# The mixers' weight splits: ACT's negative and an adding DMA in place of a subtraction on DVE and GpSimd

## The chip, the cores and the metric

The kernel runs on one core of a Trainium2 chip. The metric is the device time of one execution in microseconds. One core has TensorE (PE, matrix multiplication; its weight loads are shown as PEld), VectorE (DVE), ScalarE (ACT), GpSimd (POOL) and SyncE (SP), each with its own instruction queue that is worked off in order. SP and POOL also issue DMA transfers, which sixteen DMA engines carry out.

## The reference, cut to what matters

The program is the trunk of a small decoder with 512 tokens of width 1024 and two layers. Each layer is: half a SwiGLU feed-forward block, a token mixer, half a SwiGLU block, all with RMSNorm before and after.

```
h = h + 0.5 * post(SwiGLU_a(pre(h)))
h = h + post(Mixer(pre(h)))
h = h + 0.5 * post(SwiGLU_b(pre(h)))
even layer: proj = u @ w_in  ->  dilated attention heads | gated DeltaNet heads  ->  @ w_out
odd  layer: proj = u @ w_in  ->  conv, SiLU, Mamba-2 chunked scan, gate, norm    ->  @ w_out
```

All data are float32. The change touches only how the weights of the two input projections `u @ w_in` are prepared.

## The kernel before, in words

**Products in split form.** TensorE multiplies in float32r, which keeps fewer bits than float32. So every operand is held as two parts, `hi` (the value rounded to float32r) and `lo` (the rest, value minus `hi`), and each product is three matmuls: hi·hi, hi·lo and lo·hi. One unit of weights is a tile of 128 partitions by 1024 numbers, 512 KB. `weights` (L88) takes such a unit through these steps: SP loads it from HBM into a tile `wraw` (`load`, L83; three buffers); ACT casts it into `whi` (L80); DVE subtracts, `wlo = wraw - whi` (L81). `whi` and `wlo` come from the pool `wsplit` with four buffers each. `product` (L159) then issues 24 matmuls for the unit, three for each of the eight blocks of rows (L167, L168, L169); the third of the first three, L169, is the first that needs `wlo`. A `wraw` buffer is free for the next load when the subtraction has read it; a `wsplit` buffer when the unit's last matmul is done.

**Sharing with GpSimd.** In the even mixer, from `self.share = True` (L899) to the end of the heads, every fifth subtraction goes to GpSimd instead of DVE.

**The even mixer** (L578 on) computes, between L899 and L929, the attention heads as a filler between the steps of the gated DeltaNet heads: 20 units of weights. Its longest serial piece is `invert32` (L693), 31 steps of a small multiplication and a reduction, both on DVE (L718, L719), by which a triangular matrix is inverted; meanwhile PE works at the attention (transposes L847 and L853, scores L831 and L832) and at further projections.

**The odd mixer** (L936 on) goes through four groups `g`. For each it projects B and C, then four blocks `i` of x, and then four gate blocks z: ten units, except that the first four units are made earlier, so 36 units in the loop. A projection ends in `conv_silu` (ACT L474, three DVE steps L476, ACT's tanh L478, DVE L479). For each block of x two decay tiles `M` (256 KB each) are read from a row in HBM by DMAs that **POOL** issues (L557), ACT works on them (L1062, L1065 four times, L1066), DVE multiplies (L1067), and PE takes them in L1072. There are four `M` buffers, so the loads for block `i+2` wait until PE is through with L1072 of block `i`. The transposes of a block of x into tokens are L1006.

**What sets the order.** The code is written stage by stage; a scheduler of the framework orders the instructions of each engine by priority and by its own estimate of when they can run, when the kernel is built. The order of each queue is then fixed.

Of the kernel before, what the change touches and what calls it, by code (L numbers as in the profile page):

```python
# [9 lines left out]
F32 = mybir.dt.float32  # L10
# [3 lines left out]
AF = mybir.ActivationFunctionType  # L14
OP = mybir.AluOpType
# [15 lines left out]
class Trunk:  # L31


    def __init__(self, ctx, tc, norm_w, tables, out):
        self.tc, self.nc, self.norm_w, self.tables, self.out = tc, tc.nc, norm_w, tables, out
        nc = self.nc
        pool = lambda name, **kw: ctx.enter_context(tc.tile_pool(name=name, **kw))
        self.consts = pool("consts", bufs=1)
        self.resid = pool("resid", bufs=1)
        self.wraw = pool("wraw", bufs=3)  # L40
        self.wsplit = pool("wsplit", bufs=4)
        self.scr = pool("scr", bufs=2)
        self.small = pool("small", bufs=4)
        self.dram = pool("dram", bufs=1, space=bass.MemoryType.DRAM)
        self.psum_mm = pool("psum_mm", bufs=2, space=bass.MemoryType.PSUM)
        self.psum_ctx = ctx.enter_context(ExitStack())
        self.banks({"acc": 4, "tr": 2})

        self.share, self.n_weights = False, 0
        self.ident = self.consts.tile([128, 128], F32, name="ident")  # L50
        make_identity(nc, self.ident)
        self.warm(24)
        self.h = self.resid.tile([128, TT, D], F32, name="h")
        self.uT = [self.resid.tile([128, TT, KD, 128], F32R, name=n) for n in ("uhi", "ulo")]
# [19 lines left out]
            return self.psum_mm.tile([128, 512], F32, name=tag)  # L74
        return self.psum.tile([128, 512], F32, name=tag, bufs=self.tags[tag])

    def split(self, src, hi, lo, on_pool=False):

        nc = self.nc
        nc.scalar.copy(hi, src)  # L80
        (nc.gpsimd if on_pool else nc.vector).tensor_tensor(lo, src, hi.bitcast(F32), op=OP.subtract)  # L81

    def load(self, src, shape):  # L83
        raw = self.wraw.tile([128] + shape, F32, name="wraw")
# [3 lines left out]
    def weights(self, src, shape, parts=None, raw=None):  # L88

        nc = self.nc  # L90
        raw = self.load(src, shape) if raw is None else raw
        hi, lo = parts or [self.wsplit.tile([128] + shape, F32R, name=x) for x in ("whi", "wlo")]
        self.n_weights += 1
        self.split(raw, hi, lo, self.share and self.n_weights % 5 == 0)
        return hi, lo

    def w_cols(self, w, c0, n=128, raw=None):
# [474 lines left out]
    def even_mixer(self, w_in, conv_w, a_log, dt_bias, head_norm_w, w_out, post_w, next_pre):  # L572
        nc, tc = self.nc, self.tc
# [7 lines left out]
        with ExitStack() as ctx:  # L581
# [314 lines left out]
                finish(*waiting)  # L896
                yield 1.5

            self.share = True  # L899
            fill = attention()  # L900
            for need in gated_delta():
                while need > 0:
# [23 lines left out]
                            nc.sync.dma_start(self.h[:, i, :], hd[i])  # L926
                    yield

            self.share = False  # L929
            parts.close()  # L930
            self.out_product(ctx, lambda t, k, half: [u[:, t, k, :] for u in self.uT], w_out, KD, 1.0, post_w, next_pre,
                             before=gates(pool("even_z", bufs=2)))
# [3 lines left out]
    def odd_mixer(self, w_in, conv_w, conv_b, dt_bias, a_log, d_skip, out_norm_w, w_out, post_w, next_pre):  # L936
        nc, tc = self.nc, self.tc
# [10 lines left out]
        with ExitStack() as ctx:  # L948
# [29 lines left out]
            with tc.tile_pool(name="odd_t", bufs=1, reuse_waits="tile") as tp:  # L978
                first = (DI // 128, DI // 128 + NG, 0, 1)
                ps, raw = self.first_products(w_in, [X0 + j * 128 for j in first], "acc",  # L980
                                              lambda: self.small_product(tp, w_in[:, DT0:DT0 + NH], NH, ("acc", "tr")))
# [11 lines left out]
            def project(j, tag="feat", bufs=2):  # L993
                p = first.get(j)
                if p is None:
                    p = self.ps("mm")
                    self.product(p, self.w_cols(w_in, X0 + j * 128))
                o = gp.tile([128, T], F32, name=tag, bufs=bufs)
                self.conv_silu(p, [cw[:, k * nconv + j:k * nconv + j + 1] for k in range(4)],
                               cw[:, 4 * nconv + j:4 * nconv + j + 1], o, gp)  # L1000
                return o
# [7 lines left out]
            def rstd_cols(g, sq):  # L1009

                p = self.ps("tr")[:, :TT]
                for t in range(TT):
                    nc.tensor.matmul(p[:, t:t + 1], sq[:, t * 128:(t + 1) * 128], self.ones[:, :1], start=True, stop=True)
                ss = self.small.tile([128, TT], F32, name="ssy")
                nc.vector.tensor_copy(ss, p)
                rms[g] = self.rstd(ss, 4 * GW, 0.5)
# [11 lines left out]
                    self.split(blocks(y[:, i, :]), *(o[:, :, g % 2 * NB + i, :] for o in (early if g < 2 else self.uT)))  # L1028

            ready, rms = {}, {}  # L1030
            for g in range(NG):
                Bf, Cf = project(DI // 128 + g), blocks(project(DI // 128 + NG + g, "Cf", 2))
                bt = gp.tile([128, TT, 128], F32, name="bt")
# [64 lines left out]
                for i in range(NB):  # L1098
# [7 lines left out]
                    if i:  # L1106
                        tt(sq, sq, th, op=OP.add)
                ready[g] = y
            rstd_cols(NG - 1, sq)

            for g in (NG - 2, NG - 1):
# [7 lines left out]
def kernel(  # L1119
# [29 lines left out]
    for layer in range(depth):  # L1149
        ffn = [(ffn_w_gate[layer, i], ffn_w_up[layer, i], ffn_w_down[layer, i]) for i in range(2)]  # L1150
        mixer, weights = (k.odd_mixer, odd) if layer % 2 else (k.even_mixer, even)
        k.ffn(*ffn[0], (layer, 1), (layer, 2), *(() if layer else (raws,)))
        mixer(*(w[layer // 2] for w in weights), (layer, 3), (layer, 4))
        k.ffn(*ffn[1], (layer, 5), (layer + 1, 0) if layer + 1 < depth else None)
# [47 lines left out]
```

## Time and profile before

| | |
|---|---|
| median of 3 runs | 2156.76 us (2154.38 to 2159.07) |
| the profiled execution | 2155.31 us, of which the span from the first to the last instruction 2153.5 us |
| PE busy | 2112.7 us (98%) |
| DVE busy | 1479.1 us (69%) |
| ACT busy | 1026.2 us (48%) |
| POOL busy | 149.5 us (7%) |

Matmuls are pipelined, and the busy time counts them with overlapping ends, so PE's 98% says that PE rarely waits long, and not that it runs at its peak. What another engine's change can win is the time in which PE stands still for it.

### The profile page before, as it was taken

What the parts mean: (1) busy time and instruction counts of PE and PEld (TensorE: products, weight loads), DVE (VectorE), ACT (ScalarE), POOL (GpSimd) and SP (SyncE); (2) the same over time, 40 slices, a digit from 0 to 9 for tenths busy, and PEclk for the clock granted to TensorE, in tenths of its full rate; (3) what the DMA queues carried; (4) which work ended last, traced back from release to release, by engine and by line L of the source; (5) the groups of instructions that cost most, each with busy time, mean ns of one, the idle gap of its engine ahead of it and who ended that gap; (6) DMA issues with size and microseconds to landing.
All of it is one profiled execution on the core that took longest, in us unless ns stands there. A gap on an engine that the chain in (4) does not pass through costs nothing.

```text
span 2153.5 us, 33163 instructions
## 1 busy us (share of the span) xinstructions
PE 2112.7 (98%) x13311; PEld 1871.1 (87%) x13311; DVE 1479.1 (69%) x2329; ACT 1026.2 (48%) x1577; POOL 149.5 (7%) x142
## 2 busy tenths in 40 slices
PE   8999999999999999999999999999999999999998
PEld 7999988887788999988899998877778788999986
DVE  5866656869667767656686765668888846867653
ACT  4544543455563454534344455347565423544541
POOL 0011000111200011000001100000000000011000
PEclk9999999999999999999999999999999999999999
DMA  8687334342323687533658642324334236586321
GB/s 235 148 195 167 118 100 135 101 126 66 88 70 117 158 205 176 127 118 98 157 138 196 157 132 94 101 74 118 98 90 126 69 118 157 142 196 157 122 89 68
DMA packets 284037, 277.06 MB, mean 129 GB/s; under 512 B 18576, under 2 KB 244552, under 8 KB 283884
## 3 DMA queue, kind: packets, MB, share of 16 engines
q1 hardware_dynamic: 243308, 228.81, 35.0%
q0 software_dynamic: 40576, 46.14, 13.0%
q8 instruction: 104, 1.70, 0.3%
q14 instruction: 49, 0.40, 0.1%
HBM read 265.93 MB, written 4.79 MB: 126 GB/s over the span
## 4 chain that ended last, share of the span: by engine, by line
PE 84%; DVE 7%; DMA 4%; ACT 3%; issue 1%; SPq 0%; POOL 0%; DVEq 0%; ACTq 0%; POOLq 0%
PE mm L300 18%; PE acc L300 13%; PE acc L235 9%; PE acc L237 9%; PE acc L236 9%; PE mm L169 4%; PE mm L168 4%; PE mm L167 4%; DMA wraw<-in_ffn_w_up_dram 2%; DMA M<-rows_o 1%; PE acc L649 1%; DVE wlo L81 1%; PE tr L154 1%; PE acc L169 1%; PE acc L167 1%
## 5 line engine op out<-in xcount | busy, mean ns | idle before, releaser
L80 ACT CAST whi<-wraw 128x1024 fp32r<-128x1024 f32 x296 | 310.0, 1049 | 400.0 <-PE acc L237 107.4
L81 DVE TENSOR_TENSOR wlo<-wraw,whi 128x1024 fp32r<-128x1024 f32 x292 | 356.5, 1223 | 143.4 <-ACT whi L80 141.6
L167 PE MATMUL mm<-uhi,whi 128*128 128x512 f32 (+1 forms) x736 | 274.1, 373 | 1.6 <-DVE feat L476 1.3
L168 PE MATMUL mm<-ulo,whi 128*128 128x512 f32 (+1 forms) x736 | 272.9, 371 | 0.2 <-DVE ulo L81 0.2
L169 PE MATMUL mm<-uhi,wlo 128*128 128x512 f32 (+1 forms) x736 | 271.5, 369 | 0.0
L80 ACT CAST whi<-wq 128x1024 fp32r<-128x1024 f32 x144 | 150.8, 1049 | 241.4 <-issue 77.4
L81 DVE TENSOR_TENSOR wlo<-wq,whi 128x1024 fp32r<-128x1024 f32 x144 | 175.4, 1222 | 96.7 <-ACT whi L80 96.6
L235 PE MATMUL acc<-whi,hs 128*128 128x512 f32 x576 | 227.3, 395 | 0.0
L236 PE MATMUL acc<-wlo,hs 128*128 128x512 f32 x576 | 227.2, 394 | 0.0
L380 POOL DMA_DIRECT2D wq<-in_ffn_w_up_dram x72 | 92.7, 1290 | 1074.3 <-DMA wq<-in_ffn_w_gate_dram 404.0
L300 PE MATMUL mm<-uhi,whi 128*128 128x256 f32 x576 | 163.8, 284 | 3.2 <-DVE q L388 3.1
L300 PE MATMUL mm<-uhi,wlo 128*128 128x256 f32 x576 | 163.0, 283 | 0.0
L300 PE MATMUL mm<-ulo,whi 128*128 128x256 f32 x576 | 163.0, 283 | 0.0
L300 PE MATMUL acc<-uhi,whi 128*128 128x256 f32 x576 | 162.8, 283 | 0.0
L300 PE MATMUL acc<-uhi,wlo 128*128 128x256 f32 x576 | 162.8, 283 | 0.0
L300 PE MATMUL acc<-ulo,whi 128*128 128x256 f32 x576 | 162.8, 283 | 0.0
L167 PEld LDWEIGHTS mm<-uhi,whi 128*128 128x128 f32 x736 | 139.1, 189 | 26.3 <-issue 2.9
L168 PEld LDWEIGHTS mm<-ulo,whi 128*128 128x128 f32 x736 | 139.4, 189 | 25.2 <-issue 5.0
L169 PEld LDWEIGHTS mm<-uhi,wlo 128*128 128x128 f32 x736 | 139.4, 189 | 23.8 <-issue 3.6
L237 PE MATMUL acc<-whi,hs 128*128 128x512 f32 x384 | 151.5, 395 | 0.0
L236 PEld LDWEIGHTS acc<-wlo,hs 128*128 128x128 f32 x576 | 108.5, 188 | 25.3
L235 PEld LDWEIGHTS acc<-whi,hs 128*128 128x128 f32 x576 | 108.5, 188 | 25.0
(393 smaller groups left out, 5240.1 us busy)
## 6 DMA issues: line engine op xcount, KB each, us to landing
wraw<-in_ffn_w_down_dram SPq DMA_DIRECT2D x88, 512.0 KB, 3.5
wq<-in_ffn_w_gate_dram SPq DMA_DIRECT2D x72, 512.0 KB, 5.4
wq<-in_ffn_w_up_dram POOLq DMA_DIRECT2D x72, 512.0 KB, 7.6
wraw<-in_ffn_w_gate_dram SPq DMA_DIRECT2D x52, 512.0 KB, 5.4
wraw<-in_ffn_w_up_dram SPq DMA_DIRECT2D x52, 512.0 KB, 6.4
wraw<-in_odd_w_in_dram SPq DMA_DIRECT2D x40, 512.0 KB, 3.9
wq<-in_ffn_w_up_dram SPq DMA_DIRECT2D x36, 512.0 KB, 3.8
wraw<-in_even_w_in_dram SPq DMA_DIRECT2D x28, 512.0 KB, 4.3
```

Source lines behind the costliest of these rows:

```text
L80: nc.scalar.copy(hi, src)
L81: (nc.gpsimd if on_pool else nc.vector).tensor_tensor(lo, src, hi.bitcast(F32), op=OP.subtract)
L154: nc.tensor.transpose(p[:, j * 128:(j + 1) * 128], u[:, k * 128:(k + 1) * 128], self.ident)
L167: nc.tensor.matmul(p, whi[:, k, :], hi, start=k == 0, stop=False)
L168: nc.tensor.matmul(p, whi[:, k, :], lo, start=False, stop=False)
L169: nc.tensor.matmul(p, wlo[:, k, :], hi, start=False, stop=k == KD - 1)
L235: nc.tensor.matmul(p, ahi, hi, start=k == 0, stop=False)
L236: nc.tensor.matmul(p, ahi, lo, start=False, stop=False)
L237: nc.tensor.matmul(p, alo, hi, start=False, stop=k == nk - 1)
L300: self.nc.tensor.matmul(p[:, f * 256:(f + 1) * 256].rearrange("p (t c) -> p t c", c=128), l, r, start=new and f == k == i == 0, stop=f == ...
L380: nc.gpsimd.dma_start(raw, src, accum_op=OP.add)
L649: nc.tensor.matmul(p[:, c, :], lhs[:, c, :], rhs[:, c, :], start=True, stop=True)
```

## The change

Between L899 and L929 of the even mixer and in the loop over the groups of the odd mixer, the second part of a weight unit is made in another way. ACT writes the negative of `whi` into `wlo` (a second ACT instruction, L97 of the changed kernel), and then POOL issues a DMA that adds `wraw` to `wlo` in place, from SBUF to SBUF, 512 KB (L98). No subtraction on DVE or GpSimd is left there. Elsewhere (feed-forward blocks, the first four units of each mixer, output projections) nothing is changed. The share of GpSimd goes away.

```diff
-    def split(self, src, hi, lo, on_pool=False):
+    def split(self, src, hi, lo):
         nc.scalar.copy(hi, src)
-        (nc.gpsimd if on_pool else nc.vector).tensor_tensor(lo, src, hi.bitcast(F32), op=OP.subtract)
+        nc.vector.tensor_tensor(lo, src, hi.bitcast(F32), op=OP.subtract)
@@ weights
-        self.n_weights += 1
-        self.split(raw, hi, lo, self.share and self.n_weights % 5 == 0)
+        if not self.adding:
+            self.split(raw, hi, lo)
+            return hi, lo
+        nc.scalar.copy(hi, raw)
+        nc.scalar.activation(lo, hi.bitcast(F32), AF.Copy, scale=-1.0)
+        nc.gpsimd.dma_start(lo, raw, accum_op=OP.add)
         return hi, lo
@@ even_mixer
-            self.share = True
+            self.adding = True
             fill = attention()
...
-            self.share = False
+            self.adding = False
@@ odd_mixer
             ready, rms = {}, {}
+            self.adding = True
             for g in range(NG):
...
                 ready[g] = y
+            self.adding = False
```

The scheduler makes a new order for every engine. Three places of it matter below. First DVE in the even mixer, before the split of `k` (the tile `k_...<-mm_...`) that PE waits for; a number behind a name is the buffer's. Before:

```order
L121 SCALAR_TENSOR_TENSOR rs_y_4148<-rs_t_4150,rs_y_4148 128x4
L686 SCALAR_TENSOR_TENSOR ET_4383<-ET_4383,gc_3700,trineg_3678 128x128
L115 TENSOR_TENSOR rs_t_4150<-rs_y_4148 128x4
L81 TENSOR_TENSOR wlo_4471<-wraw_4468,whi_4470 128x1024
L116 TENSOR_TENSOR rs_t_4150<-rs_t_4150,rs_x_4146 128x4
L81 TENSOR_TENSOR k_4212<-mm_4181,k_4212 128x512
```

And in the changed kernel:

```order
L119 TENSOR_TENSOR rs_t_4151<-rs_y_4149 128x4
L120 TENSOR_TENSOR rs_t_4151<-rs_t_4151,rs_x_4147 128x4
L125 SCALAR_TENSOR_TENSOR rs_y_4149<-rs_t_4151,rs_y_4149 128x4
L683 SCALAR_TENSOR_TENSOR kl_3702<-ssk_4141,rs_y_4149 128x4
L686 TENSOR_TENSOR beta_3695<-beta_3695,rs_y_4149 128x4
L686 TENSOR_TENSOR nbeta_3696<-nbeta_3696,rs_y_4149 128x4
L81 TENSOR_TENSOR k_4214<-mm_4182,k_4214 128x512
```

The weight's subtraction, two places ahead of the split of `k`, is gone; a few tiny instructions have moved ahead of the split.

Second, POOL's queue in the odd mixer, group 1. Before it holds only the loads of `M`, two for each block (the rows are those of blocks 1, 2 and 3):

```order
L557 DMA M_14820<-rows_o_13831 128x512
L557 DMA M_14829<-rows_o_13831 128x512
L557 DMA M_14916<-rows_o_13831 128x512
L557 DMA M_14925<-rows_o_13831 128x512
L557 DMA M_15006<-rows_o_13831 128x512
L557 DMA M_15015<-rows_o_13831 128x512
```

In the changed kernel (blocks 2 and 3 of the same group, and the first two loads of group 2):

```order
L98 DMA wlo_14995<-wraw_14992 128x1024
L98 DMA wlo_15112<-wraw_15109 128x1024
L98 DMA wlo_15149<-wraw_15146 128x1024
L561 DMA M_14947<-rows_o_13851 128x512
L561 DMA M_14956<-rows_o_13851 128x512
L561 DMA M_15038<-rows_o_13851 128x512
L561 DMA M_15047<-rows_o_13851 128x512
L561 DMA M_15405<-rows_o_13851 128x512
L561 DMA M_15414<-rows_o_13851 128x512
L98 DMA wlo_15187<-wraw_15184 128x1024
```

The adding DMAs share the queue with the loads of `M`; one of them (`wlo_15149`) stands directly ahead of the loads for block 2.

Third, ACT at the same place: the work on the `M` tiles of blocks 2 and 3, and the tanh (`scr<-conv`) of block 2's convolution, whose result PE transposes in L1006. Before:

```order
L1062 ACTIVATE E_14698<-M_14925 64x384
L1066 ACTIVATE M_14916<-M_14916 128x512
L1065 ACTIVATE M_14925<-M_14925,cum_13830 128x128 x4
L1066 ACTIVATE M_14925<-M_14925 128x512
L1062 ACTIVATE E_14698<-M_15006 64x384
L1065 ACTIVATE M_15006<-M_15006,cum_13830 128x128 x2
L478 ACTIVATE scr_14907<-conv_14902 128x512
```

And in the changed kernel:

```order
L1067 ACTIVATE E_14726<-M_14956 64x384
L1071 ACTIVATE M_14947<-M_14947 128x512
L1070 ACTIVATE M_14956<-M_14956,cum_13850 128x128 x4
L96 CAST whi_15186<-wraw_15184 128x1024
L482 ACTIVATE scr_14938<-conv_14933 128x512
L1071 ACTIVATE M_14956<-M_14956 128x512
L1067 ACTIVATE E_14726<-M_15038 64x384
```

The tanh stands ahead of block 3's `M` now, behind block 2's and behind a weight's cast.

## Rows read from the trace of the kernel before

**Rows 1.** Groups by line, of the page: busy us, mean ns, idle before.

```profile
L81 DVE TENSOR_TENSOR wlo<-wraw,whi 128x1024 fp32r<-128x1024 f32 x292 | 356.5, 1223 | 143.4 <-ACT whi L80 141.6
```

**Rows 2.** Windows: length, busy us (instructions) of PE, PEld, DVE, ACT, POOL; clock; DMA.

```profile
385.00:545.00 160.00, 153.94 (x882) 128.69 (x880) 130.31 (x344) 84.57 (x187) 19.72 (x12) 0.99 0.39 104
410.00:420.00 10.00, 8.04 (x52) 6.88 (x51) 10.00 (x37) 8.44 (x28) 3.11 (x1) 1.00 0.38 88
420.00:430.00 10.00, 9.34 (x66) 9.35 (x67) 8.49 (x46) 2.96 (x12) 0.00 (x0) 0.83 0.49 127
500.00:550.00 50.00, 45.99 (x253) 37.78 (x252) 48.79 (x89) 18.88 (x33) 4.91 (x3) 1.00 0.28 76
1415.00:1680.00 265.00, 254.01 (x1368) 201.43 (x1366) 217.16 (x353) 164.26 (x325) 17.24 (x32) 0.99 0.36 104
1440.00:1450.00 10.00, 8.04 (x36) 6.31 (x34) 5.54 (x6) 3.98 (x9) 2.21 (x4) 1.00 0.83 221
1450.00:1460.00 10.00, 8.61 (x42) 6.11 (x43) 3.61 (x6) 7.72 (x20) 1.07 (x2) 0.83 0.34 93
```

**Rows 3.** PE's waits, 352 to 690 and 1420 to 1705 us: total, times, longest.

```profile
PE mm L198 <- DVE k L81: 2.6, 2, 2.4
...
PE tr L1006 <- DVE rs_y L121: 4.5, 3, 1.8
PE acc L1072 <- DVE M L1067: 3.4, 1, 3.4
PE tr L544 <- DVE ld_a L534: 1.9, 1, 1.9
```

**Rows 4.** Instructions of tiles wlo, whi and M in both stretches: ns min/median/max.

```profile
L81 DVE TENSOR_TENSOR wlo<-wraw,whi x16: 1203/1220/1226, 396.2 to 536.2; 128x1024 fp32r<-128x1024 f32 x16
L81 POOL TENSOR_TENSOR wlo<-wraw,whi x4: 2382/2402/3106, 391.0 to 499.8; 128x1024 fp32r<-128x1024 f32 x4
L80 ACT CAST whi<-wraw x37: 1029/1047/1057, 1417.0 to 1676.9; 128x1024 fp32r<-128x1024 f32 x37
L557 POOL DMA_DIRECT2D M<-rows_o x32: 539/539/583, 1440.6 to 1665.1; - x32
```

**Rows 5.** Timeline of DVE and PE, even mixer: start, length, idle before.

```profile
416.53 1.22 DVE L81 TENSOR_TENSOR wlo<-wraw,whi 128x1024 fp32r<-128x1024 f32 x1
419.93 0.68 DVE L81 TENSOR_TENSOR k<-mm,k 128x512 fp32r<-128x512 f32 x1
420.66 0.39 PE L198 MATMUL mm<-whi,uhi 128*128 128x256 f32 x1 [2.38 <-DVE k L81]
```

**Rows 6.** The chain that ended last, 498 to 552 us: its pieces on weights.

```profile
512.59 1.12 DVE wlo L81
531.34 1.13 DVE wlo L81
536.26 1.13 DVE wlo L81
546.93 1.22 DVE wlo L81
```

**Rows 7.** Odd mixer, start of group 0: DVE, SP's queue, the chain.

```profile
1439.81 3.49 DVE L81 TENSOR_TENSOR wlo<-wraw,whi 128x1024 fp32r<-128x1024 f32 x3
...
1441.05 4.42 SPq L85 DMA_DIRECT2D wraw<-in_odd_w_in_dram  x3
...
1441.21 8.21 DMA M<-rows_o
```

**Rows 8.** DMA queues (packets, MB, share of 16 engines) and issues (us to landing).

```profile
q1 hardware_dynamic: 243308, 228.81, 35.0%
q0 software_dynamic: 40576, 46.14, 13.0%
...
wq<-in_ffn_w_up_dram POOLq DMA_DIRECT2D x72, 512.0 KB, 7.6
...
M<-rows_o POOLq DMA_DIRECT2D x32, 256.0 KB, 3.8
```

**Rows 9.** Timeline, odd mixer: three casts on ACT, and PE's use of the first.

```profile
1470.79 2.92 ACT L80 CAST whi<-wraw 128x1024 fp32r<-128x1024 f32 x3
...
1478.78 0.48 PE L169 MATMUL mm<-uhi,wlo 128*128 128x512 f32 x1
```

**Rows 10.** Timeline of ACT and PE in group 1, block 2.

```profile
1523.54 0.53 ACT L1062 ACTIVATE E<-M 64x384 f32<-64x384 f32 x1 [1.03 <-DMA M<-rows_o]
...
1524.55 0.61 ACT L478 ACTIVATE scr<-conv 128x512 f32<-128x512 f32 x1
...
1526.04 0.63 PE L1006 MATMUL tr<-ident,feat 128*128 128x128 f32 x4 [1.58 <-DVE rs_y L121]
```

More of the change, by code (lines that the diff above doesn't have):

```diff
@@ L47, in __init__ @@
         self.banks({"acc": 4, "tr": 2})
-        self.share, self.n_weights = False, 0
+        self.adding = False
         self.ident = self.consts.tile([128, 128], F32, name="ident")
@@ L1108, in odd_mixer @@
                 ready[g] = y
+            self.adding = False
             rstd_cols(NG - 1, sq)
```

## The prediction

> **What bounds the kernel now.** I read the page first: the split of `wlo` on DVE is among its costliest groups, 292 pieces of 1.22 us [rows 1]. Then the windows of the two stretches that the change touches. Neither DVE nor ACT is full over a whole stretch: in the even one (160 us) PE is busy for 153.9, DVE 130.3 and ACT 84.6; in the odd one (265 us) PE 254.0, DVE 217.2 and ACT 164.3 [rows 2]. So PE stands still for 6.1 and 11.0 us, 17 us in all, 0.8% of the time, and no change of the splits can win much more. DVE's busy share is what can mislead here: it is 81 and 82%, but only where PE waits for DVE is it worth time.
>
> Next, PE's waits. In the even stretch the longest is 2.4 us for the split of `k` on DVE; in the odd one 4.5 us in three waits of the transposes L1006, 3.4 in one of L1072 for the first `M`, and 1.9 for the decay [rows 3]. A long wait costs twice: behind the 2.4 us wait the window 420 to 430 has a granted clock of 0.83, behind the 3.4 us wait the window 1450 to 1460 too, both next to windows at 1.00 [rows 2]. Taking 0.83 as part of the window at 1.2 and the rest at 2.4 GHz, each dip loses about 10 x 0.17 = 1.7 us. Last I followed the timelines around these waits and the chain through the inversion.
>
> **What the change moves.** Units: the even stretch has 16 subtractions on DVE of 1.22 us and 4 on POOL of 2.4; the odd one has 37 casts and subtractions [rows 4], 36 of them in the loop. DVE is relieved of 16 x 1.22 = 19.5 us and 36 x 1.22 = 43.9 us. ACT gets 20 and 36 more instructions of the cast's size; I take the cast's 1.05 us [rows 4]: 21.0 and 37.8 us, which brings it to 105.6 of 160 and 202.1 of 265. POOL gets 56 DMA issues; the 128-row loads of `M` take 0.54 us each there [rows 4], so 30 us, and loses 4 x 2.4.
>
> *The adding DMA itself* is not in this trace. The nearest are the feed-forward block's 72 adding DMAs, from HBM and with shorter rows. Their engine time: queue q0 took 13.0% of 16 x 2153.5 us, 4479 us; its 32 loads of `M` are 8.4 MB, at q1's rate (35.0%, 12060 us for 228.8 MB, 52.7 us per MB) 442 us; the rest, 4037 us for 37.7 MB, is 107 us per MB, or 3.5 us on all 16 engines for 512 KB [rows 8]. A plain transfer of that size takes 1.7. I take 3.5 (it adds, as they do), with 1.7 as the lower bound. To landing they take 7.6 us in a stretch with far busier DMA engines, the `M` loads 3.8 [rows 8]; I take 5.5, between the two.
>
> *Is `wlo` late for PE?* The chain after a cast was a subtraction of 1.2 us; now it is 1.05 (negative) + 0.54 + 5.5 = 7.1 us, up to 9.2 with 7.6. The tightest units are the three casts in a row from 1470.79, the first of which ends at about 1471.8 and is used at 1478.78, 7.0 us later [rows 9]. The others have more cover, since four buffers let ACT run ahead. So one or two waits of up to 2 us; I count 0, upper bound 4.
>
> *Even mixer, the wait for k.* The subtraction at 416.53 stands 1.22 us in DVE's queue ahead of the split of `k` at 419.93, for which PE waits 2.38 us, and DVE is full in that window, 10.00 of 10 [rows 2, 5]. The new order has none there, and earlier ones leave the same full stretch. Gain 2.4 (lower bound 0, upper 4.1 with the clock's dip).
>
> *Even mixer, the inversion.* The chain from 498 to 552 us runs through DVE and has four weight subtractions in it, 4.6 us, of which the last belongs to an unchanged unit [rows 6]; 3.4 us leave. PE stands still for 4.0 us between 500 and 550 [rows 2]. Gain 3.0 (0 to 4.0).
>
> *Odd mixer, the start.* The wait of 1.9 us for the decay has one subtraction ahead of it: gain 1.2 (0 to 1.9). Then `M`: three subtractions, late on DVE from 1439.81, free three `wraw` buffers, so three loads start at 1441.05, together with the first loads of `M`, whose landing takes 8.21 us instead of 3.8 [rows 7, 8]; the DMA engines are 0.83 busy in that window [rows 2]. With the second parts made on ACT and by DMA the buffers come free one by one, before that. 4.4 us of landing against a wait of 3.4 [rows 3]: gain 3.4 (0 to 5.1 with the dip).
>
> *Odd mixer, groups 1 to 3.* The three waits of L1006, 4.5 us, are not DVE's doing, though the last releaser named is a small DVE step. ACT's tanh for block 2 runs only at 1524.55, because the queue has block 3's `M` ahead of it, which ACT waits 1.03 us for; PE gets its transposes at 1526.04 [rows 10]. This chain is PE's L1072, POOL's issue, the landing, ACT, and a lighter DVE does not shorten it. The new order puts the tanh one `M` earlier in group 1, but puts an adding DMA on POOL directly ahead of the loads for block 2, in the same queue. The load is 0.36 of the DMA engines over this stretch now [rows 2]; 36 x 3.5 = 126 us of 265 add 0.48, so 0.84. I take 1 us more per group, a loss of 3.0 (from a gain of 4.5, if the waits go, to a loss of 13, if the landing goes to 8.2 in each).
>
> The Trainium skill bears on this place: the page "DMA: Bandwidth & Descriptors", section "Issuing engines are not separate DMA queues", says that transfers from SP, ACT and POOL run on the same sixteen engines and interleave. By that rule the new transfers slow the `wraw` loads and the `M` loads alike, and the 8.21 us landing in the 0.83 window agrees.
>
> Sum: -2.4 - 3.0 - 1.2 - 3.4 + 3.0 = -7.0 us on the profiled execution's 2155.3, so 2148.3; the median of the runs lies 1.5 us higher, and I put the forecast at **2149 us**.
>
> **The rivals.**
> 1. *More is won* (chance 0.10). The dips of the clock go too (3.4 us) and the L1006 waits with them (4.5, in place of a loss of 3): 2156.8 - 7.0 - 3.4 - 7.5 = 2139. For it: DVE is 0.82 full and feeds the convolutions too. Against: rows 10.
> 2. *The loads of M become the bound* (slower, 0.24). Adding DMAs and `wraw` loads keep the engines over 0.8 busy, and the six pairs of `M` loads of blocks 2 and 3 in groups 1 to 3 land in 8.2 us, as the one pair did that ran beside three loads, and not 3.8: 6 x 4.4 = 26 us, less about 1 us of new cover each, is +20, against the other gains of 10: 2167. At half of it, 2157. It decides once the landing grows by more than about 3 us a pair. For it: rows 7; against: the mean load of 0.84 leaves gaps, and `M` is half the size.
> 3. *ACT gives back what DVE gains* (no change, 0.13). The 59 us of negatives stand in the same queue as the tanh and `M` steps; at three or four places a cast or negative of 1 us that waits for a load or for POOL delays them by 2 us: +7, so 2157. Against: ACT stays under 0.77 in both stretches.
> 4. *POOL cannot write its descriptors* (slower, 0.05). While DVE works on two operands in SBUF, POOL's issue waits for its end: up to 1.2 us for a subtraction, 0.7 for the other large steps. At 0.7 for each of two loads in nine pairs, 13 us: 2162. Against: the 32 issues of `M` took 539 to 583 ns, with DVE at 0.82 [rows 2, 4]; no such wait is seen.
>
> [...]
>
> The forecast itself has 0.48. A measurement here tells a change of about 0.2%, 4.3 us, from none; the forecast is 0.35% faster. Its own range, 2143 to 2155, holds mostly faster times and some of no change (0.43 and 0.05 of its 0.48). With rival 1, faster has 0.53; no change has 0.05 of the forecast, rival 3's 0.13 and the mild cases of rival 2 (0.05), 0.23; slower has the rest of rival 2 (0.19) and rival 4, 0.24. The range over all of them with 2 in 10 left out: 2139 to 2163.
>
> **What the profile after would show.** Right: in the even and odd stretches no DVE subtraction of `wraw`; 56 more ACT instructions of about 1.05 us; the 2.38 us wait for `k` gone or under 1.2; the first `M` landing in about 4 us, PE's wait of 3.4 gone and no 0.83 window behind it; between 500 and 550 PE busy for over 48 us. The landing of the adding DMAs near 5.5 us, and PE's third matmul seldom waiting for a DMA. Wrong: PE waiting for `wlo` from a DMA in many units, `M` landing above 6 us in the median, ACT idle for a `wraw` load with tanh behind it, or POOL's issues far above 0.54 us.

## The result and the profile after

The changed kernel is **slower**: 2183.25 us, median of 4 runs (2179.87 to 2184.11), against 2156.95 for the kernel before in the same session; ratio 1.012, 95% interval 1.0102 to 1.0137. The forecast was 2149 us with a range from 2139 to 2163. The profiled execution has a span of 2182.3 us.

First the page of the changed kernel: busy times, DMA queues, and the landing of the adding DMA.

```profile
PE 2121.4 (97%) x13311; PEld 1874.4 (86%) x13311; DVE 1421.7 (65%) x2277; ACT 1076.4 (49%) x1633; POOL 186.7 (9%) x194
...
q0 software_dynamic: 48640, 75.51, 20.0%
...
wlo<-wraw POOLq DMA_DIRECT2D x56, 512.0 KB, 5.4
```

What the change does, it does: DVE has 57 us less work, ACT 50 more. Queue q0 tells what the adding DMAs take: 20.0% of 16 x 2182.3 us is 6983 us, 2504 more than before [rows 8], and over 56 transfers and 16 engines **2.8 us of all sixteen engines each**.

Windows of the changed kernel (length, busy us of PE, PEld, DVE, ACT, POOL; clock; DMA share):

```profile
385.00:545.00 160.00, 147.94 (x806) 120.38 (x807) 105.64 (x323) 99.27 (x202) 25.61 (x27) 0.98 0.69 157
385.00:555.00 170.00, 157.63 (x884) 129.86 (x885) 114.22 (x335) 101.57 (x206) 28.30 (x30) 0.98 0.70 158
500.00:550.00 50.00, 46.48 (x237) 36.79 (x237) 48.97 (x117) 30.39 (x53) 9.16 (x9) 1.00 0.60 135
1413.00:1720.00 307.00, 282.01 (x1515) 221.03 (x1514) 196.29 (x344) 201.85 (x372) 48.63 (x68) 0.97 0.66 154
1460.00:1470.00 10.00, 7.90 (x37) 5.22 (x36) 3.82 (x6) 8.78 (x23) 1.09 (x2) 0.83 0.12 37
1490.00:1500.00 10.00, 9.84 (x44) 7.78 (x42) 2.90 (x5) 3.14 (x6) 0.00 (x0) 1.00 1.04 253
```

And of the kernel before, for comparison:

```profile
385.00:555.00 170.00, 161.62 (x913) 134.27 (x911) 139.30 (x362) 88.19 (x195) 22.36 (x14) 0.99 0.39 103
1413.00:1720.00 307.00, 296.01 (x1568) 233.59 (x1567) 250.04 (x410) 178.13 (x345) 17.24 (x32) 0.99 0.35 100
```

The DMA engines go from 0.39 and 0.35 to about 0.69 and 0.66. In the even stretch PE is busy for 147.9 of 160 us where it was for 153.9 [rows 2]; in the odd stretch it stands still for 25 us of 307, where it did for 11. Over either stretch DVE and ACT are far from full, so neither's amount of work is the bound.

PE's waits (even mixer, 352 to 720 us, then odd, 1420 to 1735):

```profile
PE acc L647 <- DVE kT L483: 3.7, 2, 2.1
PE mm L171 <- DVE feat L480: 3.4, 2, 1.7
...
PE mm L202 <- DVE k L81: 0.2, 1, 0.2
...
PE mm L171 <- DVE conv L480: 7.9, 5, 2.4
PE tr L1010 <- DVE feat L483: 5.5, 5, 1.4
PE tr L548 <- DVE ld_a L538: 3.6, 1, 3.6
PE mm L171 <- DVE zth L1108: 3.1, 1, 3.1
PE tr L1010 <- DVE rs_y L123: 2.7, 1, 2.7
PE acc L1077 <- DVE M L1072: 2.1, 1, 2.1
```

The wait for `k` is gone as forecast (0.2 us, was 2.4 [rows 3]). What has grown is `mm L171`: the first matmul of a product waits until DVE has read a PSUM tile of an earlier projection. In the odd mixer of the kernel before, no row names it. No row has PE waiting for `wlo`. Part of what holds DVE up stands on ACT, whose waits for DMAs are shown here from 1425 to 1715 us, and in the last row from 352 to 720:

```profile
ACT E L1067 <- DMA M<-rows_o: 20.9, 6, 5.8
...
ACT M L1070 <- DMA M<-rows_o: 13.8, 6, 5.3
ACT whi L96 <- DMA wraw<-in_odd_w_in_dram: 11.6, 3, 6.4
...
ACT whi L96 <- DMA wraw<-in_even_w_in_dram: 5.1, 1, 5.1
```

The transfers that it waits for land later. DMA issues of the changed kernel and then of before, 1413 to 1720 us (KB each, median us to landing):

```profile
wraw<-in_odd_w_in_dram SPq DMA_DIRECT2D x33, 512.0 KB, 5.2
M<-rows_o POOLq DMA_DIRECT2D x32, 256.0 KB, 4.7
```

```profile
wraw<-in_odd_w_in_dram SPq DMA_DIRECT2D x33, 512.0 KB, 3.9
```

ACT's longest wait of 6.4 us, in the timeline of the changed kernel (SP's queue, ACT, PE), and two pieces of the chain that led to the cast:

```profile
1487.46 9.58 SPq L85 DMA_DIRECT2D wraw<-in_odd_w_in_dram  x3
...
1497.59 1.05 ACT L96 CAST whi<-wraw 128x1024 fp32r<-128x1024 f32 x1 [6.38 <-DMA wraw<-in_odd_w_in_dram]
...
1501.47 0.57 ACT L1107 ACTIVATE zth<-mm 128x512 f32<-128x512 f32 x1
...
1502.94 0.50 PE L171 MATMUL mm<-uhi,whi 128*128 128x512 f32 x1 [3.11 <-DVE zth L1108]
...
1482.78 4.62 DMA wlo<-wraw
...
1487.46 10.11 DMA wraw<-in_odd_w_in_dram
```

The first row folds three weight loads into one; they start at 1487.46, 1493.38 and 1496.67. The first starts when an adding DMA has landed, since that frees its `wraw` buffer. It then takes 10.11 us, with two more adding DMAs beside it and the DMA engines full (1.04 in the window 1490 to 1500). ACT's queue has the cast of this load at its head and stands still for 6.38 us; behind it is `zth`, which reads a PSUM tile. There are only two such tiles (`mm`), so PE stops for 3.11 us.

### The profile page after: what moved, and what is told of

Same layout as the page of the kernel before. It is cut to its first block, busy times and chain, and to the rows that moved or that the text cites. A ratio compares the mean times of both kernels' runs of the same rounds, so it can differ in the third digit from the quotient of the medians.

```text
span 2182.3 us, 33299 instructions
## 1 busy us (share of the span) xinstructions
PE 2121.4 (97%) x13311; PEld 1874.4 (86%) x13311; DVE 1421.7 (65%) x2277; ACT 1076.4 (49%) x1633; POOL 186.7 (9%) x194
## 4 chain that ended last, share of the span: by engine, by line
PE 80%; DMA 6%; DVE 6%; ACT 4%; issue 3%; POOL 0%; SPq 0%; DVEq 0%; POOLq 0%; ACTq 0%
PE mm L304 18%; PE acc L304 13%; PE acc L239 9%; PE acc L240 9%; PE acc L241 9%; PE mm L171 4%; PE mm L172 4%; PE mm L173 4%; DMA M<-rows_o 2%; DMA wraw<-in_ffn_w_up_dram 2%; PE acc L653 1%; ACT M L1070 1%; PE acc L173 1%; PE acc L171 1%; PE acc L172 1%
## 5 line engine op out<-in xcount | busy, mean ns | idle before, releaser
L80 ACT CAST whi<-wraw 128x1024 fp32r<-128x1024 f32 x240 | 251.8, 1049 | 356.2 <-PE acc L241 111.3
L81 DVE TENSOR_TENSOR wlo<-wraw,whi 128x1024 fp32r<-128x1024 f32 x240 | 293.4, 1222 | 135.2 <-ACT whi L80 133.4
L171 PE MATMUL mm<-uhi,whi 128*128 128x512 f32 (+1 forms) x736 | 275.0, 375 | 14.9 <-DVE conv L480 7.9
L171 PEld LDWEIGHTS mm<-uhi,whi 128*128 128x128 f32 x736 | 139.9, 191 | 43.5 <-ACT wlo L97 6.4
```

What stands on the lines that cost most here:

```text
L81: nc.vector.tensor_tensor(lo, src, hi.bitcast(F32), op=OP.subtract)
L171: nc.tensor.matmul(p, whi[:, k, :], hi, start=k == 0, stop=False)
```

## The experiments

**Which mixer.** e1 has the adding DMA in the even mixer alone (`self.adding` stays off in the odd loop), e2 in the odd one alone.

> The adding DMA in the even mixer alone; the odd mixer splits on DVE as before. From the profiles, PE reaches the same matmul 8.6 us later at the end of the even stretch and another 19.7 us later at the end of the odd one. If the losses are each mixer's own: about 2157 + 9 = 2166 us, and in the odd stretch the waits of before. Rival (one mixer's loss comes from the other, or from the new order elsewhere): under 2160 or over 2175.

> The adding DMA in the odd mixer alone. Each mixer's own loss: about 2157 + 20 = 2177 us, and the even stretch as before but for the GpSimd share, which is off. Rival: under 2170.

e1: 2164.06 us, ratio 1.0048 (1.003 to 1.0065). e2: 2172.23, 1.0078 (1.005 to 1.0107). Each mixer loses for itself, 8 to 10 and 17 us; together that is the whole loss. (e2 lies between its forecast and its rival's limit.)

**ACT or the transfer.** My first theory was that raw buffers, held until the adding DMA lands, starve ACT. e3 keeps the negative and lets DVE add; e4 adds from HBM, so that the raw tile is free after the cast; e6 shrinks the transfer; e7 and e8 take the negative off ACT; e5 prices the GpSimd share.

```diff
e3: -  nc.gpsimd.dma_start(lo, raw, accum_op=OP.add)
    +  nc.vector.tensor_tensor(lo, raw, lo.bitcast(F32), op=OP.add)
e4: +  nc.gpsimd.dma_start(lo, src, accum_op=OP.add)
e6: +  nc.gpsimd.dma_start(lo[:, :1, :], raw[:, :1, :], accum_op=OP.add)
e7: -  nc.scalar.activation(lo, hi.bitcast(F32), AF.Copy, scale=-1.0)
    +  nc.gpsimd.tensor_scalar(lo, hi.bitcast(F32), -1.0, None, op0=OP.mult)
e8: +  nc.vector.tensor_scalar(lo, hi.bitcast(F32), -1.0, None, op0=OP.mult)
e5: (kernel before)  self.share = False throughout
```

> ACT still writes the negative into wlo, but DVE adds the loaded weights instead of the DMA: ACT's load of the changed kernel with no adding DMA, and a raw buffer that is free about 2.5 us after the cast. Theory (raw buffers held by the adding DMA, and its traffic): 2157 to 2164 us, ACT waits for raw weights under 3 us in the odd stretch. Rival (the second ACT instruction in ACT's queue is the cause): over 2172 us.

> The adding DMA reads the weights again from HBM instead of from the raw tile, so a raw buffer is free when ACT has cast it; ACT's work, the adding DMAs and their bytes stay. Theory (a raw buffer held until the adding DMA lands makes the loads late, and ACT's queue waits for them): ACT's waits for raw weights in the odd stretch fall from 11.6 to under 3 us, and the time to 2155 to 2168 us. Rival (the adding DMAs' traffic slows the M tiles and small loads): 2180 us or more, since the rows are shorter and the DMA engines still busier.

> The kernel before with the GpSimd share off, so that DVE makes all subtractions: the part of the change that e2 and e3 contain too. The profile of e2 stood 6.4 us ahead at the inversion of the even mixer and gave 2.7 of it back. If the share's removal is worth that alone: 2151 to 2154 us. If not, within 3 us of before.

> The changed kernel with the adding DMA over one of the eight blocks of a unit only (the rest of the second part stays the bare negative): ACT's work and the DVE relief stay, the adding traffic falls to an eighth and a raw buffer comes free sooner. Theory ACT (e3: the second ACT instruction delays what stands behind it): 2170 us or more. Theory DMA (traffic and held buffers): under 2162 us.

> The negative on GpSimd instead of ACT, the adding DMA kept in full: ACT's queue is that of before, DVE is relieved, the adding DMAs wait for POOL. Theory ACT: under 2162 us. Theory DMA: 2170 us or more, with ACT's waits for raw weights and for M as in the changed kernel; a slow POOL instruction (over 2 us) ahead of the loads of M would also show there.

> The negative on DVE, the adding DMA kept in full: no additional ACT work. If DVE's one-operand instruction takes half of the subtraction, DVE is relieved by half. Theory ACT: 2150 to 2162 us. Theory DMA: 2170 us or more.

| | us | ratio (95%) |
|---|---|---|
| e3 ACT's negative, DVE adds | 2175.12 | 1.0095 (1.0061 to 1.0129) |
| e4 adds from HBM | 2183.98 | 1.013 (1.0093 to 1.0167) |
| e5 no share | 2152.07 | 0.9984 (0.9963 to 1.0005) |
| e6 short transfer | 2153.31 | 0.9996 (0.9981 to 1.0011) |
| e7 negative on GpSimd | 2201.26 | 1.022 (1.0188 to 1.0252) |
| e8 negative on DVE | 2190.55 | 1.0166 (1.0142 to 1.019) |

e4 missed its theory's range: the raw tiles come free early, ACT's casts in the loop no longer wait for their loads (11.6 us in the changed kernel), and yet nothing is won. ACT's waits for `M` rise from 34.7 to 43.9 us instead; e4 moves shorter rows, and its DMA engines are 0.82 busy in the window 1413 to 1720, where the changed kernel's are 0.66. So held buffers alone are not the cause. e6 has all of ACT's 56 negatives and no loss; e7 and e8 have none of them and the full loss or more. So in the changed kernel ACT's additional work is not the cause, the transfer is. e3 does not fit either theory: it loses some 20 us with no transfer, in a kernel whose DVE is not relieved. e7 adds its own price, a slow instruction on POOL ahead of the DMAs; e8's negative costs DVE little more than half of a subtraction (rows of e7 and of e8):

```profile
L97 POOL TENSOR_SCALAR wlo<-whi x36: 2759/2767/3474, 1436.1 to 1729.5; 128x1024 fp32r<-128x1024 f32 x36
```

```profile
L97 DVE TENSOR_SCALAR wlo<-whi x36: 682/692/699, 1430.2 to 1710.5; 128x1024 fp32r<-128x1024 f32 x36
```

**Queue, traffic or held buffers.** e9 moves the loads of `M` to SP's queue. e10 to e12 take e6 and add two plain copies per unit that nobody reads.

```diff
e9:  -  self.row_bcast(m..., rows, h, nc.gpsimd)
     +  self.row_bcast(m..., rows, h, nc.sync)
e10: +  for _ in range(2):
     +      nc.gpsimd.dma_start(<a new HBM tile>, hi.bitcast(F32))
```

e11 has the copies of e10 issued by SP, e12 has them read the raw tile.

> The changed kernel with the loads of M issued by SP, on the queue of the weight loads, instead of POOL behind the adding DMAs. Theory queue (an M load stands behind an adding DMA in POOL's queue and lands late): M lands in about 4 us, the odd mixer loses under 10 us instead of 20, 2165 to 2174 us. Theory engines (sixteen shared DMA engines are filled, whatever the queue): within 5 us of the changed kernel, 2183. It can also come out worse, where an M load waits behind a weight load on SP.

> The kernel with the short adding DMA (e6, 2153 us), and for each unit two plain copies of whi, 512 KB each, to HBM, issued by POOL and read by nobody: the traffic of the full adding DMA (2 x 1.6 us of the engines for 2.6) and its place in POOL's queue, but raw buffers come free early and no second part is late. Theory traffic or queue: 2170 to 2185 us. Theory held buffers or late second parts: under 2160 us.

> As e10, with the copies issued by SP: the same traffic, and nothing large ahead of M in POOL's queue. Theory queue: clearly under e10, below 2165 us. Theory engines: within 5 us of e10.

> As e10, with the copies reading the raw tile, so that a raw buffer is held until they have landed, as by the full adding DMA. What it takes over e10 is the price of the held buffers alone: theory held buffers 10 us or more, theory traffic under 4.

e9: 2189.57, 1.014 (1.0114 to 1.0166). e10: 2181.65, 1.0115 (1.0085 to 1.0145). e11: 2178.13, 1.0091 (1.0071 to 1.0112). e12: 2195.47, 1.0179 (1.015 to 1.0207). The queue that issues makes no difference that can be told: e10 and e11 are 3.5 us apart. e9 lies outside both of its ranges: against the kernel before in its own session it is 5 us slower than the changed kernel, with intervals that overlap, and it wins nothing. The Trainium skill's rule cited in the prediction ("DMA: Bandwidth & Descriptors", section "Issuing engines are not separate DMA queues") agrees with e9 to e11. e12's 14 us over e10, at the same engine time, point to held buffers as a cost of their own, but e12 has another order of the queues, so this pair alone does not isolate it.

**Order or transfers.** The scheduler makes a new order for each kernel, so the loss could lie in the order. It can be pinned: at the end of the kernel each instruction gets an edge to the one that is to stand ahead of it on its engine, which sets the order and adds no wait.

```diff
+    pin_order(tc)    # for each engine, a list of instructions taken from another build:
+    #   tc.add_manual_dep(i, name_of_the_one_ahead, <NoSync>)
```

e13 is the changed kernel in e6's order; e14 is e6 in the changed kernel's order; e15 is e3 in e6's order; e16 is the kernel before in its own order, with e10's copies.

> The instructions of the changed kernel, full adding DMAs, with the order of every engine's queue pinned to that of e6 (short adding DMA, 2153 us). The scheduler had made e6's order for short transfers. Theory traffic (the transfers themselves cost the time on the chip): 2175 us or more. Theory order (the scheduler's new order for long transfers costs it): under 2162 us.

> The reverse: the short adding DMA of e6 with the order of every queue pinned to that of the changed kernel. Theory traffic: 2150 to 2160 us, as e6. Theory order: 2172 us or more. Something of both: the two differences from e6 add up to about 28 us.

> e3 (ACT's negative, DVE adds, no DMA; 2175 us) with the order of PE, ACT, SP, POOL and DVE pinned to e6's, only DVE's adds placed by the scheduler. If e3's loss came from its order: under 2162 us. If ACT's second instruction ahead of DVE's add costs it on the chip: 2170 us or more.

> The kernel before in its own order on PE, ACT, DVE and SP, and for each of the 56 units two plain copies of whi to HBM, issued by POOL, read by nobody. No second part is late, no raw buffer is held, no order is changed there: only traffic and POOL's queue. Theory traffic: 2172 us or more. Theory order or late second parts: under 2162 us.

| | transfer | order | us | ratio (95%) |
|---|---|---|---|---|
| changed kernel | full | its own | 2183.25 | 1.012 (1.0102 to 1.0137) |
| e13 | full | e6's | 2188.68 | 1.0157 (1.013 to 1.0184) |
| e14 | short | the changed kernel's | 2150.17 | 0.9967 (0.9948 to 0.9986) |
| e6 | short | its own | 2153.31 | 0.9996 (0.9981 to 1.0011) |
| e16 | idle copies | that of before | 2183.33 | 1.0153 (1.0108 to 1.0198) |
| e15 | none, DVE adds | e6's | 2176.35 | 1.0098 (1.0068 to 1.0129) |

This settles order against transfer. With either order the full transfer costs 33 to 35 us, and the changed kernel's order costs nothing. e16 shows that traffic is enough to lose time: its copies make no second part late and hold no raw buffer, no cast waits for a copy, and PE, ACT, DVE and SP keep their order. (POOL's queue has the copies in it; by e10 and e11 that makes no difference that can be told.) Its q0, and ACT's waits in its odd mixer:

```profile
q0 software_dynamic: 56704, 104.87, 19.8%
```

```profile
ACT M L1071 <- DMA M<-rows_o: 24.9, 10, 10.5
ACT E L1068 <- DMA M<-rows_o: 19.0, 10, 3.4
...
ACT whi L81 <- DMA wraw<-in_odd_w_in_dram: 8.8, 3, 4.7
```

19.8% of 16 x 2198.9 us is 6966 us, 2487 more than before: the same engine time as the adding DMAs, and a loss of 27 us. The profiled execution was the longest of its four, 2200.65 us, so these waits are somewhat larger than in the median run. e14 is the counterpart, with the changed kernel's order and little traffic. Its windows, ACT's waits for DMAs (1413 to 1720 us), PE's waits (1390 to 1700 us), and the place of the 6.38 us wait:

```profile
385.00:555.00 170.00, 165.01 (x952) 136.93 (x950) 119.80 (x352) 110.56 (x226) 31.11 (x32) 1.00 0.49 117
500.00:550.00 50.00, 46.10 (x252) 37.32 (x251) 44.52 (x85) 24.80 (x46) 10.25 (x10) 1.00 0.47 106
1413.00:1720.00 307.00, 298.54 (x1583) 235.56 (x1582) 217.86 (x377) 212.17 (x384) 48.62 (x68) 0.99 0.42 110
```

```profile
ACT E L1067 <- DMA M<-rows_o: 10.4, 7, 3.1
ACT M L1070 <- DMA M<-rows_o: 10.0, 6, 3.7
ACT whi L96 <- DMA wraw<-in_odd_w_in_dram: 0.2, 1, 0.2
```

```profile
PE mm L171 <- DVE conv L480: 5.0, 3, 2.3
PE tr L1010 <- DVE feat L483: 1.8, 3, 1.2
PE acc L1077 <- DVE M L1072: 1.6, 1, 1.6
```

```profile
1472.02 0.41 ACT L1070 ACTIVATE M<-M,cum 128x128 f32<-128x128 f32 x1 [1.95 <-DMA M<-rows_o]
1472.33 1.04 ACT L96 CAST whi<-wraw 128x1024 fp32r<-128x1024 f32 x1
```

The same cast in the same place of the same queue does not wait for its load here, and it runs 25 us earlier. ACT's waits for DMAs in the odd mixer are 20.6 us against 46.3, and PE is busy for 298.5 of 307 against 282.0, in the even window for 165.0 of 170 against 157.6. These two differences are 23.9 of the 33 us; the granted clock, 1.00 and 0.99 against 0.98 and 0.97, gives another 0.02 x 477 = 9.5 us, a rough estimate since the shares are rounded. It falls behind long waits: the window 1460 to 1470 of the changed kernel, behind the wait for the first `M`, has 0.83, as the like window of before had [rows 2].

e15 keeps e3's loss in another order, so that loss is not the order's; it met the forecast of the theory that ACT's second instruction ahead of DVE's add costs time on the chip, but no run shows how. e5, whose DVE subtracts directly, has none of it. In e15 one cast waits 9.1 us for its load; the rest of PE's waits is spread over many places. I leave that cause open.

**Dose.** e17 replaces the adding DMA by a plain one, in the changed kernel's pinned order; e18 uses the adding DMA for every fourth unit and DVE for the others.

> The changed kernel in its own pinned order, with a plain DMA of raw into the second part, 512 KB, in place of the adding one (so the second part is the raw weights): the same number of transfers, bytes and dependencies, but about 1.6 us of the sixteen engines each for 2.6. If the loss goes with the engines' time, between e14 (0.3 us each, 2150) and the changed kernel (2.6 us, 2183) in proportion: about 2168 us, and M and raw landings between theirs. If it goes with the waits on a transfer (a late second part, a held raw buffer) at whatever length: 2178 us or more.

> A version that could beat both: the adding DMA for every fourth unit of both stretches alone, 14 in all, DVE for the others, no GpSimd share. A quarter of the traffic, by e13 and e14 a loss of up to 8 us, against 1 to 2 us for a quarter of DVE's relief and the 3 us that the share's removal showed in e5: 2150 to 2160 us. Under 2150 would make it the best; over 2162 would say that single transfers cost as much as many.

e17: 2160.60, 1.0031 (1.0016 to 1.0045). e18: 2165.38, 1.0046 (1.0029 to 1.0063). The q0 rows of e17 and of e14 give the doses:

```profile
q0 software_dynamic: 48640, 75.51, 16.4%
```

```profile
q0 software_dynamic: 48640, 50.08, 14.6%
```

As above, 1.3 us of the engines per unit in e17, and 0.6 in e14 (the expectations had taken 1.6 and 0.3, and 2.6 for the full one). So in one and the same order: 0.6 us, 2150.2; 1.3 us, 2160.6; 2.8 us, 2183.3. With these doses a straight line gives 2161 for e17; the 2168 expected went by the wrong ones. Both steps are about **15 us of time per us of engine time per unit**, 0.27 us for each us that the 56 transfers take of the engines. The loss grows with the transfer's length, not with its mere presence, and no threshold shows between the three points. In this line, though, a longer transfer also holds its raw tile longer. Other runs help to part the two. Each loss below is the difference of the two kernels' times, each against the kernel before in its own session; the engine time is that of all sixteen engines, from the q0 rows of the pages (for e11 q0 and q1):

| | raw tile held by the added transfer | engine time more, us | time more, us | us per us |
|---|---|---|---|---|
| changed kernel over e14 | yes | 123 | 32.6 | 0.27 |
| e13 over e6 | yes | 126 | 33.8 | 0.27 |
| e12 over e6 | yes | 156 | 38.7 | 0.25 |
| e16 over the kernel before | no | 155 | 26.8 | 0.17 |
| e10 over e6 | no | 161 | 24.8 | 0.15 |
| e11 over e6 | no | 157 | 21.3 | 0.14 |
| e4 over e6 | no | 197 | 30.0 | 0.15 |

So the 0.27 is not the price of traffic alone. Traffic by itself cost 0.14 to 0.17 us per us; where the raw tile, and with it the next weight load, waits for the transfer, it is 0.25 to 0.27. By this estimate some 17 to 21 of the changed kernel's 33 us are traffic, and the rest goes with the held tile. e4, e10, e11 and e12 have orders of their own, so the split is no sharper than the 5 us or so by which another order alone moves the time (e13 against the changed kernel, e6 against e14).

e18's 14 transfers, 39 us of engine time, cost 10.5 us by the 0.27, and it is 9.5 slower than before. That misses its expected range to 2160: the small dose pays about the same rate, and what DVE gains by it does not cover that. No version here beats the kernel before beyond doubt but e14, which leaves out seven eighths of the adding; e5 is not told from it.

## Why the prediction was wrong

**The relief of DVE was sized about right in sum.** The four gains of the sum, without its loss, are 10.0 us; e14, with all instructions and a fifth of the engine time, is 6.3 us faster than before (interval 3 to 11). It still adds 34 us of engine time, which cost 5 to 9 us by the rates above; by that estimate the relief alone is 11 to 15 us. In its windows PE is busy for 3.4 us more than before in the even mixer and for 2.5 in the odd one. The waits for `k` and for the decay are gone from PE's list and that for the first `M` is down to 1.6 us.

**The wait for `k` was read wrongly, and its gain came out in part by luck.** Between the subtraction at 416.53 and the split of `k` at 419.93 [rows 5] stands an instruction of 128 x 4 numbers, and in the kernel before it took 2.34 us, while GpSimd made its share of the subtractions:

```profile
416.87 3.11 POOL L81 TENSOR_TENSOR wlo<-wraw,whi 128x1024 fp32r<-128x1024 f32 x1 [23.50 <-ACT whi L80]
417.66 2.34 DVE L116 TENSOR_TENSOR rs_t<-rs_t,rs_x 128x4 f32<-128x4 f32 x1
```

The two end within 0.02 us of each other. The same line takes 0.16 us in the median of the stretch, and at most 0.18 in e5, which has no share and waits 1.5 us for `k`. In e16, which has the share, one such instruction takes 2.38 us beside GpSimd's 3.14. So 2.2 us of this wait were the price of the share, which the change also removes, and not of the subtraction that stands ahead on DVE.

**The inversion was shortened by more than forecast.** The window 500 to 550 cannot show it (PE is busy for 46.1 and 46.5 us there in e14 and the changed kernel, 46.0 before [rows 2]), since the inversion lies elsewhere in time. Its multiplications before, in the changed kernel and in e14:

```profile
L718 DVE TENSOR_TENSOR scr<-U,feat x31: 156/651/1089, 488.5 to 550.2; 128x1 f32<-128x1 f32 x1, 128x4 f32<-128x4 f32 x1, 128x9 f32<-128x9 f32 x1, 128x16 f32<-128x16 f32 x1
...
L722 DVE TENSOR_TENSOR scr<-U,feat x31: 157/664/1166, 499.0 to 551.2; 128x1 f32<-128x1 f32 x1, 128x4 f32<-128x4 f32 x1, 128x9 f32<-128x9 f32 x1, 128x16 f32<-128x16 f32 x1
...
L722 DVE TENSOR_TENSOR scr<-U,feat x31: 157/650/1161, 486.2 to 538.5; 128x1 f32<-128x1 f32 x1, 128x4 f32<-128x4 f32 x1, 128x9 f32<-128x9 f32 x1, 128x16 f32<-128x16 f32 x1
```

It takes 52 us in place of 62, where 3.4 were forecast to leave. Between 488 and 552 us the kernel before has six weight subtractions on DVE, 7.3 us, of which I counted those on the chain; and at 500.04 another small instruction takes 2.20 us beside a subtraction on GpSimd. Of these 9.5 us little is left to PE: over its whole even window it gains the 3.4. In the changed kernel it begins 13 us later than in e14, so that much is lost ahead of it.

**The odd start** came out in part. The three loads of [rows 7] begin one after the other, at 1441.05, 1442.19 and 1443.33, each behind a subtraction. In the changed kernel the first four loads of `M` land in 3.6 to 4.6 us, as forecast, and PE's wait for the first `M` falls from 3.4 to 2.1, not to nothing. The decay's wait, which e14 does not have, is 3.6 us instead of 1.9. The transposes L1006, which I said a lighter DVE does not help, wait 1.8 us in e14 (L1010) in place of 4.5 for `rs_y` alone before; but there PE waits 5.0 us for `conv`, which it did not before.

**The transfer itself was sized rightly, on the safe side.** Landing 5.4 us (5.5 forecast), 2.8 us of the engines (3.5), a load of 0.66 to 0.70 (0.84). Only POOL's issue was off, 0.86 us for 0.54. "I count 0" for a late `wlo` held: no row of PE's waits names it.

**The step that failed is the loss put against it**: "I take 1 us more per group, a loss of 3.0", bound 13. It measures 33 us, e14 against the changed kernel. I priced the traffic at one place, the `M` loads of groups 1 to 3, and put nothing against the weight loads and the even mixer, though I had written that the `wraw` loads are slowed alike. The transfer slows every other one that something waits for, and the weight loads also start later, when it has freed their buffer: weight loads in the odd stretch land in 5.2 us in place of 3.9, `M` in 4.7 in place of 3.8 (medians), and in the even mixer, where I put no cost, ACT waits 5.1 us for a weight load. And ACT's queue is worked off in order: the cast that waited 6.38 us held up `zth`, which reads one of PE's two PSUM tiles, and PE stood still for 3.11. ACT under 0.77 busy said nothing about that. "ACT idle for a `wraw` load with tanh behind it" stood among the signs of being wrong, without a price in the sum. How the 33 us divide over single waits is not shown.

**Rival 2** (2167, chance 0.24) had the direction and the cause, traffic, but too narrow a mechanism and too low a price. Its condition, a landing of `M` over 3 us longer, was not met in the median, which grew by 0.9 us (the longest of the later groups is 7.8), and the loss came all the same. **Rival 3**: e14 shows that 56 negatives on ACT lose nothing where DVE is relieved by them; e3 and e15, where it is not, lose 20 us, which stays open. That a cast waiting for a load holds up ACT's queue is what happened, and at a higher price than 7 us. **Rival 4** is not seen: the `M` loads' issues keep a median of 0.55 us.

## What to carry to other kernels

A transfer that nobody waits for is not free: find what else flows through the shared DMA engines at that time and which in-order queue has its consumer at the head. In a stretch whose loads are fetched just in time, price each us of added engine time over the whole stretch (0.14 to 0.17 us here, and 0.25 to 0.27 where the transfer also holds a buffer that the next load needs), not at the one wait that is in view; medians of landing hide it. Before a wait is put down to the large instruction ahead of it, read the length of every instruction between. To part a scheduler's new order from the edit's own cost, pin one build's order to the other's instructions and swap.

## What was not expected of the hardware

An adding DMA of 512 KB from SBUF to SBUF takes 2.8 us of the sixteen engines and lands in 5.4; a plain one of the same tiles (e17) takes 1.3 and lands in 3.6. POOL's issue of the adding one takes 0.86 us (median), of the plain one 0.53:

```profile
L98 POOL DMA_DIRECT2D wlo<-wraw x36: 845/857/1267, 1429.5 to 1708.7; - x36
```

```profile
L98 POOL DMA_DIRECT2D wlo<-wraw x36: 528/531/568, 1422.0 to 1684.1; - x36
```

In one order, three points of the loss lie on a line in engine time, from a DMA share of 0.42 to 0.66 in the odd stretch; I had expected gaps to absorb the first part of it. A DVE instruction of 128 x 4 numbers took 2.34 us instead of 0.16 while GpSimd subtracted. And a one-operand instruction over 128 x 1024 numbers took GpSimd 2.77 us, DVE 0.69 and ACT 1.05.
